# Three down-projection rounds by seven products in a two-layer hybrid decoder kernel, with the plain rounds accumulated onto the residual in PSUM

## The chip, the cores and the metric

The kernel runs on one core of a Trainium2 chip. The metric is the device time of one execution in microseconds. The kernel before took 1250.43 us (median of 3 runs, 1250.01 to 1251.3).

## What is computed

Two layers of a hybrid decoder on 528 tokens (16 meta tokens and 512 real ones), model width 1024. Each layer is an attention part (a combined input projection, forgetting attention, retention, an output projection) and a feed-forward part, which is where the change lies:

```python
hn = rmsnorm(h, ffn_norm_g)
ff = jax.nn.silu(jnp.einsum('bld,df->blf', hn, w_gate)) * jnp.einsum('bld,df->blf', hn, w_up)
return h + jnp.einsum('blf,fd->bld', ff, w_down)
```

The feed-forward width is 2816. The last layer needs the 512 real tokens only.

## The kernel before

Everything is kept transposed, with 128 features on the partitions and the tokens along the free axis: the residual is eight tiles h0 to h7 of 128x528. Each float32 matrix product is made of three: both operands are split into a rounded part (hi) and the remainder (lo), and TensorE (PE) multiplies hi by hi, hi by lo and lo by hi. A split costs one ScalarE (ACT) copy for hi and one VectorE (DVE) subtraction for lo; weights are split in the kernel as well, after their load.

The feed-forward part (`ffn`, L861) goes through the 22 blocks of 128 hidden features, f = 0 to 21, in six rounds, `ROUNDS` (L27). Blocks 0 and 1 are plain. Each later block is a `Unit` (L1055) that computes gate and up together by a seven-product scheme on 2x2 blocks: four sets of weight combinations are made from the gate tile `raw` and the up tile `fraw` (`make1` to `make4`, sums into a tile `S`), and PE consumes them in `head` (24 matmuls: 12 into a bank x, 12 into the bank pair zy), `middle` (36) and `tail` (24). At the end of `tail`, `done` (L1127) adds zy to saved parts on DVE (L1131, "done" below), applies silu, multiplies and splits the block's activation (tiles ah, al).

When a round of blocks is complete, its down projection is added to h while the next round's units run: unit by unit, one of four pairs of output tiles (p = 0 to 3). A *plain* fill (`down`, L1181) multiplies the blocks of the round straight into a PSUM tile and adds that to h on DVE (L1202, L1204). A *seven-product* fill (`Pair`, L992) halves a pair of outputs, a round and the tokens, and needs seven products d[0] to d[6] of 6 matmuls each instead of 48 matmuls. It prepares its own weight combinations on DVE (L1012, L1013, L1018, L1020 and splits), and adds six partial results to h (L1039, L1041). It also needs four combinations of the activations of the round, the *forms* 1 to 4 (`token_forms`, L963). They are stored in places that are free then: form 1 in the second half of an activation tile, forms 2 and 3 in the second halves of the x tiles (xh, xl), form 4 in sqh, sql. `SEVENTHS` (L29) names the rounds whose fill is by seven products: rounds 2 (blocks 6 to 9, filled under units 10 to 13) and 4 (blocks 14 to 17, filled under units 18 to 21). Rounds 0, 1 and 3 are plain; the last round ends the layer.

Order. PE runs in the order of the program text (`steps`). On the other engines a scheduler places the instructions at build time, earlier text first, those under `high_priority` ahead; on the chip each engine runs its list in that fixed order and an instruction that waits holds up those behind it. Weight sets are made one to five jobs ahead (`need`, L935) and held in rings of two and three buffers. PSUM has eight banks: two pairs (psd) and four single ones (psa).

"Unit f", "layer 0" and "layer 1" below are these; "stage f" is the time from the done of unit f to the done of unit f+1.

Of the kernel before, what the change touches and what calls it, by code (L numbers as in the profile page):

```python
# [16 lines left out]
NK = D // 128  # L17
# [8 lines left out]
NF = DFF // 128  # L26
ROUNDS = ((0, 2), (2, 6), (6, 10), (10, 14), (14, 18), (18, 22))  # L27
PLAIN = 2
SEVENTHS = (2, 4)  # L29
SEVEN = (0, 1, 2, 3)  # L30
HB = NK // 2
EPS = 1e-6
# [9 lines left out]
def hybrid_kernel(ctx, tc, x_t, w_in, w_fl, w_out, w_gate, w_up, w_down, vecs, b_fg, rope, decay, mask, ident, out_t):  # L42
    nc = tc.nc
# [9 lines left out]
    h = [state.tile([128, T], F32, name=f"h{k}") for k in range(NK)]  # L53
# [100 lines left out]
    def split(hi, lo, src, pinned=False):  # L154
        return [pin(f, pinned).ins for f in (nc.scalar.copy(hi, src), nc.vector.tensor_sub(lo, src, hi.bitcast(F32)))]
# [116 lines left out]
    def psum():  # L272
        return psd.tile([128, 2, 512], F32, name="psd", tag="psd")

    def psum_a():
        return psa.tile([128, 512], F32, name="psa", tag="psa")
# [584 lines left out]
    def ffn(l, st, real, last):  # L861
        QC = REAL if real else FULL
        t0 = META if real else 0
        w = (T - t0) // 2
        HC = ((t0, t0 + w), (t0 + w, T))
# [4 lines left out]
        halves, forms = {}, {}  # L870

        def two(t):
            return t[:, t0:T].rearrange("p (a b) -> p a b", a=2)
# [89 lines left out]
        def token_forms(f, u2):  # L963

            r = seventh(f)[0]
            f0 = ROUNDS[r][0]
            k = (f - f0) % 2
            first = [two(t)[:, 1] for t in acts[f0 + k]]
            if f - f0 < 2:
                halves[k] = u2  # L970
                nc.vector.tensor_sub(u2[:, 0], u2[:, 1], u2[:, 0])
                split(*first, u2[:, 0])
                forms[r, 1, k] = first
                return
            if k == 0:
                forms[r] = [tt("sqh", F32R), tt("sql", F32R)]
            (a, b), (c, d) = ([t[:, i] for i in range(2)] for t in (halves.pop(k), u2))
            four = [two(t)[:, k] for t in forms[r]]
            second, third = ([two(t)[:, 1] for t in st["x"][i]] for i in (2 + k, k))
            for n, o, x, y, (hi, lo) in ((3, b, d, b, third), (2, d, d, a, second), (4, c, c, d, four)):  # L980
                with tc.high_priority() if k and n < 4 else ExitStack():
                    nc.vector.tensor_sub(o, x, y)
                    split(hi, lo, o)
                forms[r, n, k] = hi, lo

        def form(r, n):
            return lambda k: forms[r, n, k]
# [190 lines left out]

            return add_job(load=load, make=lambda hi, lo: splits(hi, lo, t["r"][:, 0:2 * n]), n=2 * n)

        def down(j, s, m, f0, f1, banks):  # L1181

            n = f1 - f0
            ps = []

            def chunk(k):
                def go():
                    if k == 0:
                        need(j)
                        ps.append([psum_a() for _ in HC] if banks else psum())  # L1190
                    t = ps[0] if banks else [ps[0][:, b] for b in range(2)]
                    cols = QC if real and not banks else HC
                    _, hi, lo = jobs[j]["w"][0]
                    fh, fl = acts[f0 + k]
                    for i, (a, b) in enumerate(((hi, fh), (hi, fl), (lo, fh))):
                        for v, (c0, c1) in zip(t, cols):
                            nc.tensor.matmul(v[:, 0:c1 - c0], a[:, s * n + k, :], b[:, c0:c1],  # L1197
                                             start=(k == 0 and i == 0), stop=(k == n - 1 and i == 2))
                    if k == n - 1:
                        if banks:  # L1200
                            for v, (c0, c1) in zip(t, HC):
                                nc.vector.tensor_add(h[m][:, c0:c1], v[:, 0:c1 - c0], h[m][:, c0:c1])  # L1202
                        else:
                            nc.vector.tensor_add(sv(h[m], real), pv(ps[0], real), sv(h[m], real))  # L1204
                return go
            return [chunk(k) for k in range(n)]

        def own():
            return [(NK, wring("fwhi"), wring("fwlo"))]
# [1 line left out]
        steps = []  # L1211
        fills = []
        units = {}
        for r, (f0, f1) in enumerate(ROUNDS):
            for f in range(f0, f1):
# [10 lines left out]
                u = units[f]  # L1226
                p, g0, g1 = fills.pop(0)
                seven = r - 1 in SEVENTHS and p in SEVEN
                after = r - 1 in SEVENTHS and p + 1 in SEVEN or r in SEVENTHS and f == f1 - 1 and 0 in SEVEN
                if seven:  # L1230
                    pair = Pair(r - 1, p)
                    u.rest()
                    pair.rest()
                    u.last()
                    jobs[u.w3]["reach"] = 5 if after else 4
                    d, m, t = pair.steps(), u.middle(), u.tail()
                    steps += d[0] + m[:NK] + d[2] + m[NK:] + d[1] + d[3] + t[:HB] + d[4] + t[HB:] + d[5] + d[6]
                    continue
                u.rest()
                steps += u.middle()  # L1240
                j = down_job(p, g0, g1)
                jobs[j]["reach"] = 4 if after else 3
                steps += down(j, 0, 2 * p, g0, g1, not real or f < PLAIN + 2)
                u.last()
                steps += u.tail()
                steps += down(j, 1, 2 * p + 1, g0, g1, f == PLAIN)
            fills = [(p, f0, f1) for p in range(NK // 2)]
        n = f1 - f0
        js = [down_job(p, f0, f1) for p, _, _ in fills]
# [8 lines left out]
        else:  # L1258
# [22 lines left out]
            for c0, c1 in (PA, PB):  # L1281
                for m in range(NK):
                    ps = []
# [343 lines left out]
```

## Time and profile before

| | |
|---|---|
| median of 3 runs | 1250.43 us (1250.01 to 1251.3) |
| span of the profiled execution | 1248.2 us |
| outside that span, by the median | 2.2 us |
| PE busy | 1236.6 us (99%), 9387 matmuls |
| DVE busy | 1062.2 us (85%), 2033 instructions |
| ACT busy | 733.5 us (59%) |
| done of unit 9, layer 0 and layer 1 | 420.39 us, 1031.76 us |

The profiled execution's own time outside the span is not recorded; the median is taken for it. A busy time of PE counts matmuls that overlap, so 99% says that PE hardly ever stood still, not how fast it went. The granted clock (PEclk) is 1.00 where PE runs at its full clock.

### The profile page before, as it was taken

How to read it: one execution, taken by the hardware profiler on the slowest of the kernel's cores; microseconds unless marked ns; L12 is line 12 of the kernel's file. 1: busy time of each engine (PE TensorE's matmuls, PEld its weight loads, DVE VectorE, ACT ScalarE, POOL GpSimd, SP SyncE). 2: the span in 40 equal slices, each digit the busy share in tenths (PEclk: the TensorE clock that was granted, in tenths of full speed). 3: DMA queues.
4: the chain of work that ended last, by engine and by line, in shares of the span. 5: the costliest groups of instructions: out<-in, count | busy, mean ns of one | idle time of the engine just before them, and what ended most of it. 6: DMA issues, size and time to landing. Idle time of an engine off the chain costs nothing.

```text
span 1248.2 us, 24164 instructions
## 1 busy us (share of the span) xinstructions
PE 1236.6 (99%) x9387; PEld 1192.1 (96%) x9387; DVE 1062.2 (85%) x2033; ACT 733.5 (59%) x1397; POOL 294.6 (24%) x568
## 2 busy tenths in 40 slices
PE   9999999999999999999999999999999999999997
PEld 9999999999999999999999989999799999999996
DVE  7887756889997999899876877568999989998996
ACT  7767655776544555455566766567765445454554
POOL 4555655440000000000035556554400000000000
PEclk9999999999999999999999999999999999999999
DMA  6222222222433233322312222231414333333322
GB/s 238 68 77 69 78 69 85 60 85 72 133 119 102 85 102 118 103 86 85 114 65 85 63 84 75 68 94 52 141 54 135 111 102 102 100 104 102 102 69 69
DMA packets 43347, 116.25 MB, mean 93 GB/s; under 512 B 5088, under 2 KB 9952, under 8 KB 43232
## 3 DMA queue, kind: packets, MB, share of 16 engines
q1 hardware_dynamic: 42800, 114.41, 28.8%
q8 instruction: 74, 1.21, 0.4%
q14 instruction: 41, 0.34, 0.1%
q10 hardware_dynamic: 432, 0.29, 0.1%
HBM read 112.58 MB, written 2.10 MB: 92 GB/s over the span
## 4 chain that ended last, share of the span: by engine, by line
PE 90%; DVE 5%; ACT 2%; DMA 1%; issue 1%; SPq 0%; ACTq 0%; DVEq 0%
PE psd L231 28%; PE psa L953 22%; PE psd L953 15%; PE psd L1197 8%; PE psa L231 5%; PE psa L1197 3%; PE psa L452 2%; PE psa L619 2%; PE psa L549 1%; PE psa L753 1%; PE psa L789 1%; DMA raw<-w_down 1%; DVE wlo L942 1%; DVE fwlo L942 0%; PE psa L312 0%
## 5 line engine op out<-in xcount | busy, mean ns | idle before, releaser
L208 POOL TENSOR_TENSOR wlo<-raw,whi 128x128 fp32r<-128x128 f32 x488 | 254.6, 557 | 212.2 <-ACT whi L204 212.2
L231 PE MATMUL psd<-xh,whi 128*128 128x264 f32 (+1 forms) x696 | 169.7, 313 | 0.0
L231 PE MATMUL psd<-xh,wlo 128*128 128x264 f32 (+1 forms) x696 | 161.0, 301 | 0.0
L231 PE MATMUL psd<-xl,whi 128*128 128x264 f32 (+1 forms) x696 | 160.6, 300 | 0.0
L231 PEld LDWEIGHTS psd<-xh,whi 128*128 128x128 f32 x696 | 112.6, 190 | 3.3 <-ACT whi L204 0.3
L231 PEld LDWEIGHTS psd<-xh,wlo 128*128 128x128 f32 x696 | 111.1, 188 | 4.4
L231 PEld LDWEIGHTS psd<-xl,whi 128*128 128x128 f32 x696 | 111.7, 189 | 2.5
L941 ACT CAST fwhi<-raw 128x512 fp32r<-128x512 f32 (+2 forms) x88 | 66.2, 757 | 72.3 <-PE psd L953 28.7
L204 ACT CAST whi<-raw 128x512 fp32r<-128x512 f32 (+1 forms) x140 | 82.1, 612 | 32.5 <-PE psd L231 17.3
L127 POOL MEMSET kc<- 64x528 f32 x4 | 2.1, 534 | 367.5 <-PE psd L1197 367.3
L942 DVE TENSOR_TENSOR fwlo<-raw,fwhi 128x512 fp32r<-128x512 f32 (+2 forms) x88 | 75.1, 854 | 7.5 <-ACT fwhi L941 7.4
L941 ACT CAST whi<-raw 128x1024 fp32r<-128x1024 f32 (+2 forms) x72 | 56.8, 789 | 37.6 <-PE psd L953 21.1
L1117 ACT COPY e<-psa 128x264 f32<-128x264 f32 (+1 forms) x120 | 44.9, 374 | 53.5 <-PE psa L953 51.9
L953 PE MATMUL psa<-th,fwhi 128*128 128x264 f32 (+1 forms) x248 | 70.4, 284 | 0.0
L953 PE MATMUL psa<-tl,fwhi 128*128 128x264 f32 (+1 forms) x248 | 70.1, 283 | 0.0
L953 PE MATMUL psa<-th,fwlo 128*128 128x264 f32 (+1 forms) x248 | 70.1, 283 | 0.0
L953 PE MATMUL psa<-th,whi 128*128 128x264 f32 (+1 forms) x232 | 65.4, 282 | 0.0
L942 DVE TENSOR_TENSOR wlo<-raw,whi 128x1024 fp32r<-128x1024 f32 (+1 forms) x72 | 64.1, 893 | 1.5 <-ACT whi L941 1.4
L953 PE MATMUL psa<-tl,whi 128*128 128x264 f32 (+1 forms) x232 | 65.4, 282 | 0.0
L953 PE MATMUL psa<-th,wlo 128*128 128x264 f32 (+1 forms) x232 | 65.3, 281 | 0.0
L566 ACT ACTIVATE pr<-pr,nmax 128x144 f32<-128x144 f32 (+1 forms) x64 | 36.8, 575 | 45.7 <-DVE nmax L553 26.3
L941 ACT CAST fwhi<-S 128x1024 fp32r<-128x1024 f32 (+1 forms) x34 | 28.8, 846 | 34.0 <-PE psa L953 14.3
(442 smaller groups left out, 4381.7 us busy)
## 6 DMA issues: line engine op xcount, KB each, us to landing
raw<-w_in SPq DMA_DIRECT2D x54, 512.0 KB, 3.5
raw<-w_gate SPq DMA_DIRECT2D x44, 512.0 KB, 3.5
fraw<-w_up SPq DMA_DIRECT2D x40, 512.0 KB, 3.5
raw<-w_down SPq DMA_DIRECT2D x80, 256.0 KB, 3.7
raw<-w_out SPq DMA_DIRECT2D x16, 512.0 KB, 3.5
h<-x_t SPq DMA_DIRECT2D x8, 264.0 KB, 4.5
dec<-decay SPq DMA_DIRECT2D x8, 264.0 KB, 2.7
raw<-w_up SPq DMA_DIRECT2D x4, 512.0 KB, 3.9
```

The source lines that it names most:

```text
L204: pin(nc.scalar.copy(hi, job["raw"][:, c0:c1]), pinned)
L208: pin(sub(lo[:, c:c + step], job["raw"][:, c0 + c:c0 + c + step], hi[:, c:c + step].bitcast(F32)), pinned)
L231: nc.tensor.matmul(ps[1][b][:, 0:c1 - c0], w[:, wk, :], x[:, c0:c1], start=(k == 0 and i == 0), stop=(k == n - 1 and i == 2))
L452: nc.tensor.transpose(ps[:, 128 * j:128 * j + 128], src[:, o:o + 128], idt)
L549: nc.tensor.matmul(sc[0:nq, 0:c1 - c0], qq[:, q0:q0 + nq], kk[:, c0:c1], start=(i == 0), stop=(i == 1))
L566: nc.scalar.activation(pr, pr, AF.Exp, bias=nmax[0:nq], scale=-1.0, accum_out=rsum)
L619: nc.tensor.matmul(po[:, c0:SEQ], v[:, j, :], pp[:, j, META + c0:T], start=(j == 0 and i == 0), stop=(j == 4))
L941: nc.scalar.copy(hi, src)
L942: nc.vector.tensor_sub(lo, src, hi.bitcast(F32))
L953: nc.tensor.matmul(bank()[:, 0:b.shape[-1]], a[:, o + k, :], b, start=(fresh and k == 0 and i == 0), stop=(k == n - 1 and i == 2), skip_gr ...
L1117: nc.scalar.copy(self.t["e"][:, i], self.t["x"][:, 0:w])
L1197: nc.tensor.matmul(v[:, 0:c1 - c0], a[:, s * n + k, :], b[:, c0:c1], start=(k == 0 and i == 0), stop=(k == n - 1 and i == 2))
```

## The change

1. `SEVENTHS` becomes (1, 2, 4): round 1 (blocks 2 to 5) is filled by seven products, under units 6 to 9.
2. Rounds 1 and 2 now follow each other, so that the forms of round 2 would overwrite those of round 1 while round 1's last fill still reads them. For round 2, forms 2 to 4 are therefore taken out of `token_forms` and made under unit 9: steps `later_forms` stand in the program behind the last product that reads the old form (forms 2 and 3 of the first half behind d[1] and d[4], those of the second half at the done of unit 9, form 4 behind d[6]).
3. Plain fills under units (now rounds 0 and 3) are `kept`: ACT copies h into the PSUM tile first (`place`, between the two parts of `middle` for the first output and between those of `tail` for the second), the matmuls accumulate onto it, and ACT copies the sum back into h. The DVE add goes. Their matmuls now always use half the tokens each: in layer 1, where a bank takes 512 columns, that is two matmuls of 256 for each one of 512.

The core of the diff:

```diff
-SEVENTHS = (2, 4)
+SEVENTHS = (1, 2, 4)
...
-            if k == 0:
+            halves[k] = halves[k], u2
+            if r - 1 not in SEVENTHS:
+                for n in (3, 2, 4):
+                    later_form(r, n, k)
+            elif k:
+                for n in (2, 3):
+                    later_form(r, n, k)
+
+        def later_form(r, n, k):
+            (a, b), (c, d) = ([t[:, i] for i in range(2)] for t in halves[k])
+            if n == 4 and k == 0:
                 forms[r] = [tt("sqh", F32R), tt("sql", F32R)]
...
+            o, x, y = {2: (a, d, a), 3: (b, d, b), 4: (c, c, a)}[n]
+            hi, lo = [two(t)[:, k] for t in forms[r]] if n == 4 else [two(t)[:, 1] for t in st["x"][k if n == 3 else 2 + k]]
+            with tc.high_priority() if k and n < 4 else ExitStack():
+                nc.vector.tensor_sub(o, x, y)
+                split(hi, lo, o)
+            forms[r, n, k] = hi, lo
+
+        def later_forms(r, n, *ks):
+            return [lambda k=k: later_form(r, n, k) for k in ks] if r in SEVENTHS and r - 1 in SEVENTHS else []
...
+            def place():
+                ps.append([psum_a() for _ in HC] if banks else psum())
+                with tc.high_priority():
+                    if banks:
+                        for v, (c0, c1) in zip(ps[0], HC):
+                            nc.scalar.copy(v[:, 0:w], h[m][:, c0:c1])
+                    else:
+                        nc.scalar.copy(ps[0][:, :, 0:w], two(h[m]))
...
-                    cols = QC if real and not banks else HC
+                    cols = QC if real and not banks and not kept else HC
...
-                                             start=(k == 0 and i == 0), stop=(k == n - 1 and i == 2))
+                                             start=(k == 0 and i == 0 and not kept), stop=(k == n - 1 and i == 2), skip_group_check=kept)
...
+                        if kept:
+                            with tc.high_priority():
+                                if banks:
+                                    for v, (c0, c1) in zip(t, HC):
+                                        nc.scalar.copy(h[m][:, c0:c1], v[:, 0:w])
+                                else:
+                                    nc.scalar.copy(two(h[m]), ps[0][:, :, 0:w])
...
-                    steps += d[0] + m[:NK] + d[2] + m[NK:] + d[1] + d[3] + t[:HB] + d[4] + t[HB:] + d[5] + d[6]
+                    i = r if f == f1 - 1 else None
+                    steps += (d[0] + m[:NK] + d[2] + m[NK:] + d[1] + later_forms(i, 2, 0) + d[3] + t[:HB] + d[4]
+                              + later_forms(i, 3, 0) + t[HB:] + d[5] + d[6] + later_forms(i, 4, 0, 1))
...
+                (p0, d0), (p1, d1) = (down(j, s, 2 * p + s, g0, g1, b, True)
+                                      for s, b in enumerate((not real or f < PLAIN + 2, f == PLAIN)))
+                m, t = u.middle(), u.tail()
+                steps += m[:NK] + [p0] + m[NK:] + d0 + t[:HB] + [p1] + t[HB:] + d1
```

How the lists of the engines change at three places. **DVE, layer 0, around the done of unit 9.** Before, these are the last rows of stage 8 and the first of stage 9; fwlo_5958 is the lo part of the second weight set of unit 10, L1131 the done of unit 9:

```order
L1202 TENSOR_TENSOR h6_79<-psa_5859,h6_79 128x264
L1098 TENSOR_TENSOR raw_5838<-raw_5838,S_5959 128x512
L1012 TENSOR_TENSOR S_6063<-raw_6058 128x256
L1013 TENSOR_TENSOR S_6063<-S_6063,raw_6058 128x256
L1018 TENSOR_TENSOR raw_6058<-raw_6058 128x256
L942 TENSOR_TENSOR fwlo_5958<-S_5959,fwhi_5957 128x1024
L1131 TENSOR_TENSOR sg_5910<-psd_5774,e_5772 128x528
L942 TENSOR_TENSOR fwlo_6006<-raw_5846,fwhi_6005 128x512
```

Now the same weight set is fwlo_6033, and these are the rows up to it; ahead of them, after the done of unit 9 (L1142 now), stand another 12 instructions (four of 128x528, two of 128x512, six of 128x264), the done itself counted. xl, sql and L990 are forms of round 2:

```order
L1150 TENSOR_TENSOR tq_5996<-e_5834,tq_5996 128x264
L155 TENSOR_TENSOR sql_6025<-tq_5792,sqh_6024 128x264
L990 TENSOR_TENSOR tq_5591<-tq_5996,tq_5591 128x264 x2
L155 TENSOR_TENSOR al1_6001<-tq_5996,ah1_6000 128x528
L155 TENSOR_TENSOR xl3_4158<-tq_5591,xh3_4157 128x264
L155 TENSOR_TENSOR xl1_4150<-tq_5591,xh1_4149 128x264
L990 TENSOR_TENSOR tq_5996<-tq_5996,tq_5591 128x264
L1096 TENSOR_TENSOR S_6034<-S_6034,raw_5907 128x512
L155 TENSOR_TENSOR sql_6025<-tq_5996,sqh_6024 128x264
L1103 TENSOR_TENSOR fraw_5909<-raw_5907,fraw_5909 128x512
L1029 TENSOR_TENSOR raw_5915<-raw_5915 128x256
L942 TENSOR_TENSOR fwlo_6033<-S_6034,fwhi_6032 128x1024
```

The weight set stood one row ahead of the done of unit 9; it now ends with the 25th instruction from that done on.

**DVE, layer 1, around the done of unit 8.** Before, wlo_13206 is the lo part of the second weight set of unit 9:

```order
L1012 TENSOR_TENSOR S_13358<-raw_13353 128x256
L1013 TENSOR_TENSOR S_13358<-S_13358,raw_13353 128x256
L1018 TENSOR_TENSOR raw_13353<-raw_13353 128x256
L1204 TENSOR_TENSOR h4_77<-psd_13179,h4_77 128x512
L942 TENSOR_TENSOR wlo_13206<-S_13207,whi_13205 128x1024
L1131 TENSOR_TENSOR sg_13224<-psd_13107,e_13105 128x512
```

Now it is wlo_13515; two instructions, the done of unit 8 (L1142) and an add of 128x512, stand ahead of these rows:

```order
L1024 TENSOR_TENSOR S_13422<-S_13422,raw_13417 128x256
L1052 TENSOR_TENSOR h5_78<-psa_13356,h5_78 128x256
L1144 SCALAR_TENSOR_TENSOR sg_13488<-sg_13488,R_12068 128x512
L942 TENSOR_TENSOR fwlo_13421<-S_13422,fwhi_13420 128x512
L1095 TENSOR_TENSOR S_13516<-fraw_13411 128x512
L1147 SCALAR_TENSOR_TENSOR tq_13492<-sg_13488,R_12068 128x512
L1096 TENSOR_TENSOR S_13516<-S_13516,raw_13409 128x512
L1052 TENSOR_TENSOR h6_79<-psa_13554,h6_79 128x256
L1149 TENSOR_TENSOR tq_13492<-psa_13323,tq_13492 128x256
L1150 TENSOR_TENSOR tq_13492<-e_13336,tq_13492 128x256
L1103 TENSOR_TENSOR fraw_13411<-raw_13409,fraw_13411 128x512
L942 TENSOR_TENSOR wlo_13515<-S_13516,whi_13514 128x1024
```

It moved from one row ahead of the done of unit 8 to the 14th instruction from that done on.

**ACT, layer 1, under unit 15 (a plain fill).** Before, from the silu of unit 14 on:

```order
L441 ACTIVATE sg_14362<-sg_14362 128x512
L1117 COPY e_14409<-psa_14396 128x256
L155 CAST ah6_14370<-tq_14366 128x256
L1117 COPY e_14409<-psa_14396 128x256
L941 CAST fwhi_14509<-S_14511 128x1024
L941 CAST whi_14479<-raw_14475 128x1024
L155 CAST ah6_14370<-tq_14366 128x256
L1117 COPY e_14409<-psa_14396 128x256
```

Now, with the copies of h into PSUM (L1204) and back (L1227) for the fill's two outputs h2 and h3:

```order
L441 ACTIVATE sg_14671<-sg_14671 128x512
L1204 COPY psd_14776<-h2_75 128x2x256
L1128 COPY e_14729<-psa_14716 128x256
L941 CAST fwhi_14844<-S_14846 128x1024
L155 CAST ah6_14679<-tq_14675 128x256
L1128 COPY e_14729<-psa_14716 128x256
L941 CAST whi_14801<-raw_14797 128x1024
L155 CAST ah6_14679<-tq_14675 128x256
L1128 COPY e_14729<-psa_14716 128x256
L1227 COPY h2_75<-psd_14776 128x512
L1204 COPY psd_14842<-h3_76 128x2x256
```

The second output's copy into PSUM stands right behind the first output's copy back; both outputs use the same pair of banks.

More of the change, by code (lines that the diff above doesn't have):

```diff
@@ L974, in token_forms @@
                 return
-            if k == 0:
-                forms[r] = [tt("sqh", F32R), tt("sql", F32R)]
[L977 to L984, printed above, removed]
+            halves[k] = halves[k], u2
[8 more added lines that the diff above has]
+            if n == 4 and k == 0:
+                forms[r] = [tt("sqh", F32R), tt("sql", F32R)]
+            o, x, y = {2: (a, d, a), 3: (b, d, b), 4: (c, c, a)}[n]
[6 more added lines that the diff above has]
+            return [lambda k=k: later_form(r, n, k) for k in ks] if r in SEVENTHS and r - 1 in SEVENTHS else []
         def form(r, n):
@@ L1179, in down_job, with down @@
             return add_job(load=load, make=lambda hi, lo: splits(hi, lo, t["r"][:, 0:2 * n]), n=2 * n)
-        def down(j, s, m, f0, f1, banks):
+        def down(j, s, m, f0, f1, banks, kept=False):
             n = f1 - f0
             ps = []
+            def place():
[6 more added lines that the diff above has]
+                        nc.scalar.copy(ps[0][:, :, 0:w], two(h[m]))
             def chunk(k):
@@ L1189, in go @@
                         need(j)
-                        ps.append([psum_a() for _ in HC] if banks else psum())
+                        if not kept:
+                            ps.append([psum_a() for _ in HC] if banks else psum())
                     t = ps[0] if banks else [ps[0][:, b] for b in range(2)]
-                    cols = QC if real and not banks else HC
+                    cols = QC if real and not banks and not kept else HC
                     _, hi, lo = jobs[j]["w"][0]
@@ L1197, in go @@
                             nc.tensor.matmul(v[:, 0:c1 - c0], a[:, s * n + k, :], b[:, c0:c1],
-                                             start=(k == 0 and i == 0), stop=(k == n - 1 and i == 2))
+                                             start=(k == 0 and i == 0 and not kept), stop=(k == n - 1 and i == 2), skip_group_check=kept)
                     if k == n - 1:
-                        if banks:
+                        if kept:
[5 more added lines that the diff above has]
+                                    nc.scalar.copy(two(h[m]), ps[0][:, :, 0:w])
+                        elif banks:
                             for v, (c0, c1) in zip(t, HC):
@@ L1205, in chunk @@
                 return go
-            return [chunk(k) for k in range(n)]
+            steps = [chunk(k) for k in range(n)]
+            return (place, steps) if kept else steps
         def own():
```

4 lines of the change are left out of this document (removed).

## The prediction

> **What bounds the kernel now.** I read the page first, then the feed-forward stages by windows, then the lists of PE and DVE in order of time. The busy line and the chain by engine:
>
> ```profile
> PE 1236.6 (99%) x9387; PEld 1192.1 (96%) x9387; DVE 1062.2 (85%) x2033; ACT 733.5 (59%) x1397; POOL 294.6 (24%) x568
> ...
> PE 90%; DVE 5%; ACT 2%; DMA 1%; issue 1%; SPq 0%; ACTq 0%; DVEq 0%
> ```
>
> PE sets the end, so fewer or cheaper matmuls should show in full as long as nothing else falls behind. Whether it does is read by stage. Three windows of layer 0, from done to done: units 6 and 7 (plain fills), units 8 and 9 (plain fills, and the forms of round 2), units 10 to 13 (seven-product fills). After the length, each pair of columns is an engine's busy time and its count, PE, PEld, DVE, ACT, POOL; then the clock:
>
> ```profile
> 372.21:404.34 32.13, 32.13 (x267) 32.13 (x266) 25.68 (x43) 14.41 (x23) 0.00 (x0) 1.00 0.33 99
> 404.34:436.54 32.20, 32.20 (x267) 32.20 (x266) 32.14 (x62) 16.49 (x31) 0.00 (x0) 1.00 0.28 83
> 436.54:497.89 61.35, 61.35 (x506) 61.35 (x505) 60.98 (x107) 31.75 (x49) 0.00 (x0) 1.00 0.33 105
> ```
>
> PE is busy throughout; but in the second and the third row DVE is too: 32.14 of 32.20 and 60.98 of 61.35 us. DVE has room only under plain fills without forms (6.4 us in the first row). Both engines are full, and the change takes from one and gives to the other in the very stages 6 to 9.
>
> **Part 1: matmuls.** The spacing of matmuls, from the first and the last of runs of 264 columns (28 matmuls), of 256 (36) and of 512 (8):
>
> ```profile
> 445.82 0.28 PE L953 MATMUL psa<-th,fwhi 128*128 128x264 f32 x1
> ...
> 449.11 0.29 PE L953 MATMUL psa<-th,fwhi 128*128 128x264 f32 x1
> ...
> 1109.78 0.28 PE L953 MATMUL psa<-xl,fwhi 128*128 128x256 f32 x1
> ...
> 1113.91 0.28 PE L953 MATMUL psd<-th,whi 128*128 128x256 f32 x1
> ...
> 1116.61 0.39 PE L1197 MATMUL psd<-al,whi 128*128 128x512 f32 x1
> ...
> 1118.23 0.40 PE L1197 MATMUL psd<-ah,wlo 128*128 128x512 f32 x1
> ```
>
> That is 3.29/27 = 0.122, 4.13/35 = 0.118 and 1.62/7 = 0.231 us. Layer 0: round 1 falls from 4 pairs x 48 = 192 matmuls to 4 x 42 = 168, so 24 x 0.122 = 2.9 us less. Layer 1: round 1 was 96 of 512 columns (22.2 us) and becomes 168 of 256 (19.8 us), 2.4 us less. Against that the `kept` fills of layer 1 cut 30 (round 0) and 96 (round 3) matmuls of 512 columns into two of 256 each: 126 x (0.236 - 0.231) = 0.6 us more. **PE work: -4.7 us.**
>
> **Part 2: DVE in stages 6 to 9.** DVE's price of an instruction, where it is never idle, is the step from one start to the next:
>
> ```profile
> 419.25 1.22 DVE L942 TENSOR_TENSOR fwlo<-S,fwhi 128x1024 fp32r<-128x1024 f32 x1
> 420.39 0.70 DVE L1131 TENSOR_TENSOR sg<-psd,e 128x528 f32<-128x528 f32 x1
> 421.01 0.68 DVE L942 TENSOR_TENSOR fwlo<-raw,fwhi 128x512 fp32r<-128x512 f32 x1
> 421.61 0.70 DVE L1133 SCALAR_TENSOR_TENSOR sg<-sg,R 128x528 f32<-128x528 f32 x1
> ...
> 424.40 0.42 DVE L1138 TENSOR_TENSOR tq<-psa,tq 128x264 f32<-128x264 f32 x1
> 424.75 0.42 DVE L1139 TENSOR_TENSOR tq<-e,tq 128x264 f32<-128x264 f32 x1
> 425.08 1.22 DVE L942 TENSOR_TENSOR wlo<-fraw,whi 128x1024 fp32r<-128x1024 f32 x1
> 426.22 0.42 DVE L982 TENSOR_TENSOR tq<-tq 128x264 f32<-128x264 f32 x1
> ...
> 1030.62 1.23 DVE L942 TENSOR_TENSOR fwlo<-S,fwhi 128x1024 fp32r<-128x1024 f32 x1
> 1031.76 0.68 DVE L1131 TENSOR_TENSOR sg<-psd,e 128x512 f32<-128x512 f32 x1
> 1032.36 0.68 DVE L942 TENSOR_TENSOR fwlo<-raw,fwhi 128x512 fp32r<-128x512 f32 x1
> ...
> 1033.56 0.42 DVE L942 TENSOR_TENSOR fwlo<-raw,fwhi 128x256 fp32r<-128x256 f32 x1
> 1033.89 0.68 DVE L1204 TENSOR_TENSOR h<-psd,h 128x512 f32<-128x512 f32 x1
> ```
>
> So 1.14 us for 1024 elements, 0.62 for 528, 0.60 for 512, 0.34 for 264 and for 256 (0.33 to 0.35).
>
> First the balance. A seven-product fill needs three lo parts of 512 and one of 256, four sums of 256, one add of 528 and five of 264 (3 x 0.60 + 10 x 0.34 + 0.62 = 5.8 us); a plain one a lo part of 1024 and two adds of 528 (2.4 us). Four units take 3.4 us more each, 13.7 us. In layer 0 the first two windows hold 57.8 us of DVE work; that becomes 71.5, against PE's 64.3 - 2.9 = 61.4 us. So DVE comes out about 10 us short, less what it is ahead at the start. The adds that go to ACT (two per plain fill) are freed in stages 2 to 5 and 14 to 17, where they buy a lead of a few weight sets at most, since the rings hold no more.
>
> Where it shows is read from the list. DVE cannot start on the done of a unit before PE has finished that unit's tail, so what stands behind the done in DVE's list runs after it. In layer 0 the lo part of unit 10's second weight set ends with the 25th instruction from the done of unit 9: five of 528, four of 512, fifteen of 264 or 256, one of 1024, or 3.10 + 2.40 + 5.10 + 1.14 = 11.7 us. In that time PE has, after the tail of unit 9, d[5] and d[6] (12 matmuls), the head of unit 10 (24), d[0] (6) and the two hi products (2): 44 x 0.122 = 5.4 us. Then it needs that lo part. **Stall 6.4 us.** In layer 1 the same list has eight of 512, fourteen of 256 and one of 1024 (xl of form 2 slipped ahead of the done): 4.8 + 4.7 + 1.1 = 10.6 against 44 x 0.118 = 5.2 us, **stall 5.4 us**. One unit earlier, layer 1: two instructions and the twelve rows of the second place, that is eight of 512, five of 256, one of 1024: 7.6 against 5.2 us, **stall 2.4 us**; in layer 0 there: four of 528, three of 512, one of 264, one of 1024: 5.8 against 5.4, **stall 0.4 us**. Stages 6 and 7 still make their second set in time (3.3 us behind the done in layer 0).
>
> Each stall has two handovers on top. PE's last matmul into zy to DVE's start on it, with DVE waiting for PE; and, at the end of layer 1, a DVE instruction that PE waits for and PE's start (DVE's and PE's rows):
>
> ```profile
> 436.21 0.28 PE L953 MATMUL psd<-xh,wlo 128*128 128x264 f32 x1
> ...
> 436.54 0.70 DVE L1131 TENSOR_TENSOR sg<-psd,e 128x528 f32<-128x528 f32 x1
> ...
> 1220.24 0.69 DVE L155 TENSOR_TENSOR al<-tq,ah 128x512 fp32r<-128x512 f32 x1 [0.69 <-ACT ah L155]
> ...
> 1220.99 0.39 PE L953 MATMUL psd<-al,whi 128*128 128x272 f32 x1 [0.34 <-DVE al L155]
> ```
>
> 0.33 us from the start of the last matmul, of which my sum has 0.12; 0.06 us from the end of the DVE row; and the end of a lo part is 0.08 us behind its step (1.22 against 1.14). That makes 0.35 us a stall. The four stalls are 6.7 + 5.8 + 2.8 + 0.7 = **+16.0 us**. Behind each the later sets of the unit are late by less than PE by then is, and the done of unit 10 is about as late on DVE as on PE (23 against 21.8 us), so I add nothing there. While DVE waits behind its list, ACT's hi part of the same set waits too (its sum S is ready 1.3 us ahead of the lo part); no other engine hurts.
>
> **Part 3: PE's clock after a stall.** The stalls of stage 9 leave PE idle for 4 to 5 us at a stretch. No such gap stands in the middle of this trace, but its two ends show what idleness does. After the last matmuls (first row), and from the first ones on:
>
> ```profile
> 1238.84 1.38 PE L1345 MATMUL psa<-S,ones 128*128 128x240 f32 x6
> ...
> 1240.00:1242.00 2.00, 0.21 (x2) 1.00 0.66 223
> 1242.00:1244.00 2.00, 0.00 (x0) 0.71 0.64 226
> 1244.00:1246.00 2.00, 0.00 (x0) 0.50 1.04 340
> ...
> 1.59 4.21 PE L1458 MATMUL psa<-wide,ones 128*128 128x512 f32 x9 [1.59 <-DVE wide L64]
> 5.60 0.64 PE L231 MATMUL psd<-xh,whi 128*128 128x264 f32 x2
> 6.04 0.64 PE L231 MATMUL psd<-xl,whi 128*128 128x264 f32 x2
> ...
> 7.31 0.40 PE L231 MATMUL psd<-xl,whi 128*128 128x264 f32 x2
> 7.55 0.40 PE L231 MATMUL psd<-xh,wlo 128*128 128x264 f32 x2
> ```
>
> The clock (the number behind the count) falls to half at about 1242.8, 2.6 us after PE's last work at 1240.2. At the start two matmuls of 264 take 0.44 us until about 7.2, 5.6 us after the first matmul, and 0.24 afterwards. If a stall of 4 to 5 us halves the clock and it comes back as slowly, 5.6 us pass at 0.22 instead of 0.122 us a matmul: 5.6 x 0.445 = 2.5 us lost a stall. PE is the later engine then, so nothing covers it. I take it for the two stalls of stage 9: **+5.0 us**; bounds 0 (no fall) and 7.5 (layer 1's stall of stage 8 too).
>
> [...]
>
> **Part 4: the copies on ACT.** A copy of h into PSUM is not in the trace. Its nearest rows are a cast within SBUF and a copy out of PSUM of 512 elements; the first row is the longest job that can stand ahead of it:
>
> ```profile
> L941 ACT CAST whi<-raw 128x1024 fp32r<-128x1024 f32 x32 | 33.7, 1052 | 16.3 <-PE psd L953 7.9 <-ACT whi L941 2.2 <-ACT e L1117 2.1
> ...
> L941 ACT CAST whi<-raw 128x512 fp32r<-128x512 f32 x32 | 19.9, 621 | 20.9 <-PE psd L953 13.2 <-issue 5.1 <-PE psa L1197 2.2
> ...
> L797 ACT COPY d<-psa 128x512 f32<-128x512 f32 x8 | 4.7, 582 | 1.1 <-PE psa L786 0.9
> ```
>
> So 0.58 to 0.62 us either way. ACT is 45% busy in these windows (14.41 of 32.13). The tightest place is layer 1, where both outputs use one pair of banks: copy back 0.58, copy in 0.62 and some 0.3 of handovers are 1.5 us, under the tail's 24 x 0.118 = 2.8 us. One cast of 1.05 us in front still fits. I take 0; if two casts stood in front, 0.8 us at each of six units (4, 5, 14 to 17), so 0 to +4.8. The forms of round 1 in stages 2 to 5 (16 DVE instructions of 264, 5.4 us) go where twelve adds (5.2 us) leave: 0. No DMA is added, and SP's list is as long as before.
>
> **Sum.** -4.7 + 16.0 + 5.0 = +16.3 us. The profiled span of 1248.2 becomes 1264.5, and with the 2.2 us around it the median of 1250.43 becomes **1266.7**.
>
> **Rivals.** *Stalls without a lower clock* (0.25): the idle stretches are cut by the two hi products in between and the clock stays. 1250.4 - 4.7 + 16.0 = 1261.7. For it: one end-of-program case is all that I have. *DVE hides it* (0.05): the second set of unit 10 is ready in time after all and PE keeps its 4.7 us: 1245.7. This decides if DVE has done 25 instructions within 5.4 us of the done; the rows say 11.7, and lists are not reordered on the chip, so little speaks for it. *ACT's copies come late too* (0.08): 16.3 + 4.8, 1271.5; against it ACT's idle half. *The stalls are about half as long* (0.07), since some DVE steps go faster while PE stands: 1250.4 - 4.7 + 8.0 = 1253.7. The forecast keeps 0.55, with its own range of 1263 to 1273 (a shorter return of the clock, or three falls and an ACT wait).
>
> **Chances and range.** Two cases (0.12) lie outside 1258 to 1273, and a tenth of the others with their unknowns, which leaves about 8 in 10 inside. Faster by over 0.2% (2.5 us, about what a measurement here can tell): 0.05, the second rival; within: 0.02, the short end of the fourth; slower: 0.93.
>
> **What would show it.** Right: PE waits of 4 to 7 us with DVE's fwlo L942 as releaser (or ACT's cast that waits for the same S) shortly after the done of unit 9 in both layers, a wait of some 3 us one unit earlier in layer 1, PEclk under 1.00 behind them, no PE wait at plain fills. Wrong: DVE idle in stages 8 and 9, PE at 0.122 us a matmul through them (1245.7), or waits of PE on psd or psa copies from ACT at L1218.

## The result: 1267.92 us, 1.4% slower

| | before | after |
|---|---|---|
| median | 1250.38 us (1250.01 to 1251.3) | 1267.92 us (1266.96 to 1269.03) |
| ratio, 95% interval | | 1.0141 (1.0128 to 1.0154) |
| span of the profiled execution | 1248.2 us | 1265.8 us (its own time 1267.51) |

The time was forecast at 1266.7 us. On the page after, the busy line, the clock by slices and the chain by engine:

```profile
PE 1239.5 (98%) x9561; PEld 1202.4 (95%) x9561; DVE 1079.3 (85%) x2105; ACT 779.5 (62%) x1525; POOL 293.6 (23%) x568
...
PEclk9999999999999899999999999999999998999999
...
PE 89%; DVE 7%; ACT 2%; DMA 2%; issue 0%; SPq 0%; DVEq 0%; ACTq 0%
```

These hardly differ from before: two slices of the clock show an 8, and DVE's share of the chain went from 5 to 7%. The stages tell more. The three windows of layer 0 that the prediction shows, from done to done (stages 6 and 7, stages 8 and 9, stages 10 to 13), and then the two stretches of half clock (after the length come PE, PEld, DVE, ACT, POOL, then the clock):

```profile
372.48:403.36 30.88, 30.88 (x255) 30.88 (x254) 30.64 (x59) 14.62 (x26) 0.00 (x0) 1.00 0.31 96
403.36:444.07 40.71, 33.83 (x254) 33.05 (x253) 39.29 (x77) 19.64 (x35) 0.00 (x0) 0.92 0.27 83
444.07:505.33 61.26, 61.26 (x505) 61.26 (x504) 61.04 (x105) 32.60 (x54) 0.00 (x0) 1.00 0.33 106
429.37:436.20 6.83, 5.30 (x22) 5.00 (x23) 6.83 (x13) 3.77 (x6) 0.00 (x0) 0.50 0.35 85
1050.60:1057.42 6.82, 5.98 (x26) 5.69 (x27) 6.47 (x12) 3.32 (x7) 0.00 (x0) 0.50 0.38 96
```

Stages 6 and 7 got 1.25 us shorter (32.13 before), as fewer matmuls should make them. Stages 8 and 9 got 8.5 us longer (32.20 before), and there PE is no longer the full engine: DVE works 39.29 of 40.71 us, PE 33.83. DVE's work in these four stages grew from 57.8 to 69.9 us.

Here is the place of the loss in layer 0. First PE: the last matmul before the stall, and the waits behind it; then DVE from the done of unit 9 (first row) to the lo part that PE needs, and ACT's cast that PE waits for (last row).

```profile
424.48 0.28 PE L953 MATMUL psa<-ah,fwlo 128*128 128x264 f32 x1
430.42 0.59 PE L953 MATMUL psa<-th,fwhi 128*128 128x264 f32 x1 [5.66 <-ACT fwhi L941]
430.81 0.42 PE L953 MATMUL psa<-tl,fwhi 128*128 128x264 f32 x1
431.71 0.59 PE L953 MATMUL psa<-th,fwlo 128*128 128x264 f32 x1 [0.48 <-DVE fwlo L942]
432.09 0.42 PE L953 MATMUL psa<-th,fwhi 128*128 128x264 f32 x1
432.31 0.42 PE L953 MATMUL psa<-tl,fwhi 128*128 128x264 f32 x1
```

```profile
419.66 0.71 DVE L1142 TENSOR_TENSOR sg<-psd,e 128x528 f32<-128x528 f32 x1
...
428.21 0.42 DVE L990 TENSOR_TENSOR tq<-tq 128x264 f32<-128x264 f32 x1
428.56 0.68 DVE L1096 TENSOR_TENSOR S<-S,raw 128x512 f32<-128x512 f32 x1
429.16 0.42 DVE L155 TENSOR_TENSOR sql<-tq,sqh 128x264 fp32r<-128x264 f32 x1
429.50 0.68 DVE L1103 TENSOR_TENSOR fraw<-raw,fraw 128x512 f32<-128x512 f32 x1
430.10 0.41 DVE L1029 TENSOR_TENSOR raw<-raw 128x256 f32<-128x256 f32 x1
430.44 1.21 DVE L942 TENSOR_TENSOR fwlo<-S,fwhi 128x1024 fp32r<-128x1024 f32 x1
...
429.32 1.05 ACT L941 CAST fwhi<-S 128x1024 fp32r<-128x1024 f32 x1 [0.25 <-DVE S L1096]
```

DVE is never idle from the done to the lo part; L990 and L155 are the forms. PE's wait is put down to ACT, but ACT only waits for the sum S of L1096, which stands behind the forms. From done to lo part it is 12.0 us (11.7 were summed up). Behind the wait the matmuls come every 0.22 us, not 0.12.

Measured between the starts of the last matmuls of the units' tails, in layer 0 stage 8 took 16.45 us and stage 9 24.36, where 126 matmuls without a wait take 15.36; in layer 1 stage 8 took 17.84 and stage 9 23.07, against 14.87. The excesses are 1.1 + 9.0 + 3.0 + 8.2 = 21.3 us.

### The profile page after: what moved, and what is told of

It is laid out like the page before. It is cut to its first block, busy times and chain, and to the rows that moved or that the text cites. A ratio compares the mean times of both kernels' runs of the same rounds, so it can differ in the third digit from the quotient of the medians.

```text
span 1265.8 us, 24734 instructions
## 1 busy us (share of the span) xinstructions
PE 1239.5 (98%) x9561; PEld 1202.4 (95%) x9561; DVE 1079.3 (85%) x2105; ACT 779.5 (62%) x1525; POOL 293.6 (23%) x568
## 4 chain that ended last, share of the span: by engine, by line
PE 89%; DVE 7%; ACT 2%; DMA 2%; issue 0%; SPq 0%; DVEq 0%; ACTq 0%
PE psd L231 28%; PE psa L953 24%; PE psd L953 17%; PE psd L1218 5%; PE psa L231 5%; PE psa L452 2%; PE psa L1218 2%; PE psa L619 2%; PE psa L549 1%; PE psa L753 1%; PE psa L789 1%; DMA raw<-w_in 1%; DVE fwlo L942 1%; DMA raw<-w_down 0%; DVE wlo L942 0%
## 5 line engine op out<-in xcount | busy, mean ns | idle before, releaser
L941 ACT CAST fwhi<-raw 128x512 fp32r<-128x512 f32 (+2 forms) x100 | 70.6, 714 | 52.8 <-PE psd L953 30.2
L942 DVE TENSOR_TENSOR fwlo<-raw,fwhi 128x512 fp32r<-128x512 f32 (+2 forms) x100 | 79.8, 800 | 10.6 <-ACT fwhi L941 10.3
L953 PE MATMUL psa<-th,fwlo 128*128 128x264 f32 (+1 forms) x248 | 71.5, 288 | 1.0 <-DVE fwlo L942 1.0
L953 PEld LDWEIGHTS psa<-th,fwhi 128*128 128x128 f32 x248 | 47.7, 192 | 11.0 <-ACT fwhi L941 10.6
```

The source lines that it names most:

```text
L953: nc.tensor.matmul(bank()[:, 0:b.shape[-1]], a[:, o + k, :], b, start=(fresh and k == 0 and i == 0), stop=(k == n - 1 and i == 2), skip_gr ...
```

## The experiments

Theory: VectorE has more to do in stages 8 and 9 than these last, since round 1's seven-product fills and round 2's forms meet there; the copies on ScalarE cost nothing. Rivals: the copies and the cut matmuls (e1, e2), the mere order of VectorE's list (e3), and for the five us of half clock, that they are no loss of their own (e5, e6).

**e1, the plain fills alone.**

```diff
-SEVENTHS = (1, 2, 4)
+SEVENTHS = (2, 4)
```

> Only the plain fills change: rounds 2 and 4 stay the rounds of seven products, as before, and the plain down rows are placed into PSUM and taken out of it by ScalarE. Theory (the loss is VectorE's queue behind the forms of rounds 1 and 2, the copies cost nothing): no wait of TensorE over 1 us in the feed-forward stages, granted clock 1.0 through the units; only layer 1's plain fills, cut into pairs of 256 columns, add time: 222 matmuls of 512 become 444 of 256, by the prediction's price (0.6 us for 126) about +1.1 us, so 1251.4 us. Rival (ScalarE's copies at the head and the end of a fill hold TensorE up): 96 fills of two copies with a fraction of a microsecond each, 1255 us or more, with waits on the copies (L1206 or L1229) ahead of the plain matmuls.

Measured 1254.52 us (1253.12 to 1255.58), ratio 1.003 (1.0019 to 1.0041): the forecast of 1251.4 failed. No PE wait names a copy, and layer 0's feed-forward part is as long as before to 0.1 us in every unit; so the rival falls as well. The profiled execution (1255.58 us, the longest of seven) has its excess in three places. It reaches layer 0's units 1.2 us later, by a wait in the first input projection; that differs from execution to execution (1.2 us in e4's trace too, and -0.1 to 0.8 us in the others) and is not shown to come of the edit. Layer 1's units with plain fills take 1.7 us more by the starts of their last matmuls (1.1 was forecast). And at the end of layer 1 2.6 us go, where DVE's done comes late (rows of DVE, ACT and PE):

```profile
1217.45 1.23 DVE L942 TENSOR_TENSOR fwlo<-raw,fwhi 128x1024 fp32r<-128x1024 f32 x1 [2.34 <-ACT fwhi L941]
1218.59 0.69 DVE L1142 TENSOR_TENSOR sg<-psd,e 128x512 f32<-128x512 f32 x1
...
1216.37 1.05 ACT L941 CAST fwhi<-raw 128x1024 fp32r<-128x1024 f32 x1 [2.88 <-DMA raw<-w_down]
...
1219.33 0.39 PE L953 MATMUL psd<-ah,whi 128*128 128x272 f32 x1 [1.85 <-DVE sg L1142]
```

With fewer adds, the scheduler put the next fill's lo part ahead of the done in DVE's list; it waits for ACT's cast, and that for a DMA. Behind the wait the clock halves for 3.41 us (from 1219.98), which is part of the 2.6. The changed kernel has no such wait there. So no wait shows the copies themselves as a price, but the order that the edit gives DVE's list can be one.

**e2, the third round alone.**

```diff
-                (p0, d0), (p1, d1) = (down(j, s, 2 * p + s, g0, g1, b, True)
+                d0, d1 = (down(j, s, 2 * p + s, g0, g1, b)
...
-                steps += m[:NK] + [p0] + m[NK:] + d0 + t[:HB] + [p1] + t[HB:] + d1
+                steps += u.middle() + d0 + u.tail() + d1
```

> The third round of seven products with its later forms stays, the plain fills go back to PSUM of their own and VectorE's add onto the residual. Theory: the stalls come of the forms, so they stand here as in the changed kernel, and somewhat longer, since VectorE has the adds of rounds 0 and 3 back; TensorE saves 5.3 us of matmuls (24 x 0.122 in layer 0, 24 x 0.119 less the 126 that are not cut in layer 1), the stalls take 16 to 20 us and the half clock 5: 1266 to 1271 us. Rival (the copies and the cut matmuls make the loss): the saving of the products alone, 1245 us.

Measured 1277.69 us (1276.19 to 1279.61), ratio 1.0218 (1.0202 to 1.0233). The stalls stand, and there are more of them (who waited for whom: us in total, how often, the longest):

```profile
PE psa L953 <- ACT fwhi L941: 13.1, 3, 6.1
PE psa L953 <- DVE fwlo L942: 5.3, 4, 2.2
PE psa L953 <- DVE wlo L942: 2.9, 2, 2.2
```

Earlier stages are now late as well: against the changed kernel 2.7 us in stages 5 and 6 of layer 0, and in layer 1 6.2 us in stage 5 and 4.0 in stage 7 (stage 8 is 3.1 us shorter there). So the copies on ScalarE don't make the loss, they save 10 us of it. I had the direction, but mis-sized how full VectorE is in stages 5 to 7: the forecast of 1266 to 1271 us failed.

**e3, order instead of quantity.**

```diff
-                with tc.high_priority() if self.f == PLAIN else ExitStack():
+                with tc.high_priority() if self.f in (PLAIN, 9, 10) else ExitStack():
                     nc.vector.tensor_add(s[:, HB:NK], b[:, 0:HB], b[:, HB:NK])
```

> As the changed kernel, but the second weight set of units 9 and 10 (its sums and its split, L1092 to L1096) is put ahead on VectorE, so that the forms of round 2 come behind it. Theory of quantity (VectorE has more work in these stages than the stage lasts, and what is put back is late next): the stall of unit 10 gets shorter or goes, another stands in the next sets (by the sums of measured steps up to 4.3 us in unit 9's or 3.5 us in layer 1), in all 1256 to 1263 us with less time at half clock. Theory of order (only the place of the forms ahead of that set matters): the stalls go and the products' saving is left, 1246 to 1248 us.

Measured 1270.45 us (1270.19 to 1271.22), ratio 1.016 (1.0145 to 1.0175): even slower than the change. The list of PE's waits:

```profile
PE psa L953 <- ACT whi L941: 5.3, 2, 3.0
PE psa L953 <- DVE wlo L942: 2.6, 4, 0.8
PE psa L953 <- DVE fwlo L942: 2.3, 3, 0.8
PE psd L953 <- DVE al L155: 2.0, 2, 1.4
PE psd L953 <- ACT ah L155: 1.9, 2, 1.6
```

The wait of 5.7 us is gone, but the third sets (whi, wlo) and the activations and forms themselves (ah, al) are late in its place. In layer 1 stage 9 ends 3.5 us earlier than in the changed kernel and stage 10 gives back 5.9. What is put back is late next, as quantity has it; other orders were not run. The forecast of 1256 to 1263 us failed, since I had counted the sets of weights only.

**e4 and e8, work moved to GpSimd.** e4 moves 78 instructions, e8 40 (rounds `(1,)`, units 7 to 10).

```diff
-                nc.vector.tensor_add(s[:, 2:4], r[:, 4:6], r[:, 6:8])
...
+                e = nc.gpsimd if self.r in (1, 2) else nc.vector
+                e.tensor_add(s[:, 2:4], r[:, 4:6], r[:, 6:8])
...
-                nc.vector.tensor_sub(a[:, HB:NK], a[:, HB:NK], s[:, 0:HB])
+                (nc.gpsimd if self.f in (7, 8, 9, 10, 11, 12, 13) else nc.vector).tensor_sub(a[:, HB:NK], a[:, HB:NK], s[:, 0:HB])
```

> As the changed kernel, but GpSimd does the pair sums of rounds 1 and 2 (L1023, L1024, L1029, L1031) and the difference of the fourth weight set of units 7 to 13 (L1109), which were VectorE's: some 2 to 3 us per stage leave VectorE. Theory of quantity: every set is then ready 1.5 us or more ahead of TensorE by the sums of measured steps, no wait over 1 us, no half clock, so the products' saving shows: 1245.5 to 1247 us, below the kernel before. Rival (the forms are late whatever is ahead of them, or GpSimd's 1 to 2 us for each sum puts the sets behind as far as VectorE did): waits on the sets of weights stay, 1255 us or more.

> The run with GpSimd, at a lower dose: pair sums of round 1 alone and the fourth set's difference of units 7 to 10 alone (40 instructions on GpSimd, not 78). That run showed VectorE's instructions between two SBUF tiles at 1.2 to 1.75 us, not 0.69 to 1.22, beside GpSimd's: 21 us lost again in all. If the small waits that were left there (5.6 and 7.7 us) come of GpSimd's company, half of it gives shorter ones in stages 5 to 7 and 11 to 13, but less relief in stages 8 to 10: 1255 to 1260 us. If the relief decides, the waits of stage 9 come back by 1 to 2 us per layer: 1261 to 1265 us.

e4: 1260.37 us (1260.14 to 1261.33), ratio 1.0078 (1.0061 to 1.0094). e8: 1265.03 us (1262.67 to 1267.07), ratio 1.0124 (1.0107 to 1.014). In e4 the long stalls are gone (the longest wait of a unit is 1.4 us, on `h L1054`), and the clock stays at 1.00 throughout. But ten waits of 0.3 to 1.4 us are left in the feed-forward stages. DVE's and GpSimd's rows at one place of e4 (with e4's own line numbers, two further down):

```profile
988.29 0.69 DVE L1098 TENSOR_TENSOR S<-S,raw 128x512 f32<-128x512 f32 x1
988.88 0.42 DVE L1054 TENSOR_TENSOR h<-psd,h 128x256 f32<-128x256 f32 x1
989.22 1.75 DVE L942 TENSOR_TENSOR fwlo<-raw,fwhi 128x512 fp32r<-128x512 f32 x1
990.89 0.68 DVE L942 TENSOR_TENSOR fwlo<-S,fwhi 128x512 fp32r<-128x512 f32 x1
991.49 1.21 DVE L1105 TENSOR_TENSOR fraw<-raw,fraw 128x512 f32<-128x512 f32 x1
...
989.11 1.32 POOL L1111 TENSOR_TENSOR raw<-raw,S 128x512 f32<-128x512 f32 x1 [13.51 <-ACT fwhi L941]
991.11 1.04 POOL L1033 TENSOR_TENSOR raw<-raw,S 128x256 f32<-128x256 f32 x1 [0.69 <-DVE fwlo L942]
```

A subtraction of 512 elements takes 0.68 us alone and 1.75 and 1.21 beside GpSimd, which of its 36 us of relief (64 x 0.42 + 14 x 0.68) takes 21 back (every row that overlapped GpSimd's against the median of its shape alone: 9.5 us in layer 0 and 11.5 in layer 1). So e4 supports quantity (less work, no long stall), while its own forecast of 1246 failed for a price that I had left out. e8 has its waits at wlo again (6.0 us in three, in stage 10 of both layers and stage 12 of layer 1, not in stage 9 as expected) and landed at the top of the second case, which is nearer to the relief deciding than to GpSimd's company.

**e5 and e6, the stall filled with matmuls.**

```diff
+                        v = psum_a()
...
+                            nc.tensor.matmul(v[:, 0:w], hi[:, 0, :], x, start=True, stop=True)
...
+                        d[0].append(lambda n=34 if real else 40, go=idle: go(n))
```

> As the changed kernel, with extra matmuls of 264 (256) columns into a bank that nobody reads, put right ahead of the first matmul that waits in the stage of unit 10: 40 of them in layer 0 (40 x 0.122 = 4.9 us of the 5.9), 34 in layer 1 (4.1 us of the 4.8). Theory (the idle time makes the clock fall, and the half clock is a loss of its own of 2.5 to 2.8 us per layer): the granted clock stays 1.0, the matmuls behind the wait come at 0.12 us, 1262 to 1263.5 us. Rival (VectorE stays the bound behind the wait, so that at full clock TensorE only waits again for the next sets): clock 1.0, but new waits behind, 1266 to 1268.5 us. If the idle time isn't what lowers the clock: 0.22 us spacing as before, 1268 us.

> The same with half as many extra matmuls: 20 in layer 0 (2.4 us, some 3.5 us of the wait left idle), 17 in layer 1 (2.0 us, 2.8 left). It asks how much idle time it takes: in the run without ScalarE's copies a wait of 2.5 us in layer 0 went by at full clock and waits of 2.4 us in layer 1 did not. If 2.5 to 3.5 us is enough, the clock falls in at least one layer and the time is 1264 to 1268 us; if it takes more than 3.5 us, 1262 to 1263.5 us.

e5: 1266.56 us (1265.92 to 1266.99), ratio 1.013 (1.0115 to 1.0145). PE in layer 0's stall; then stage 9 of both layers by windows:

```profile
424.68 5.00 PE L1272 MATMUL psa<-ah,fwhi 128*128 128x264 f32 x40
430.51 0.39 PE L953 MATMUL psa<-th,fwhi 128*128 128x264 f32 x1 [0.83 <-ACT fwhi L941]
...
431.79 0.39 PE L953 MATMUL psa<-th,fwlo 128*128 128x264 f32 x1 [0.78 <-DVE fwlo L942]
```

```profile
420.00:444.30 24.30, 22.70 (x184) 22.27 (x183) 24.16 (x47) 12.36 (x22) 0.00 (x0) 1.00 0.22 72
1042.00:1064.70 22.70, 21.36 (x179) 20.95 (x178) 22.64 (x44) 12.30 (x21) 0.00 (x0) 1.00 0.23 70
```

The idle time does lower the clock: with PE fed, it stays at 1.00. Stage 9 gets 2.0 and 2.3 us shorter, so the half clock cost 4.3 us where it stood. But at full clock PE meets the next limit: stage 12 of layer 1 gives back 1.2 us (a wait of 0.76 on DVE's wlo; e6 has the same). Stages 3 and 4 of layer 1, ahead of the filled stall, take 0.9 us more, with two waits of 0.2 us on ACT's copies e; why they come is not shown. By the medians 1.4 us are left of the gain, which lies in the rival's range; the theory's 1262 to 1263.5 us failed.

e6: 1268.46 us (1265.87 to 1270.55), ratio 1.0145 (1.0129 to 1.016). Layer 0 before and after the fall of the clock, and layer 1's stall:

```profile
424.80:431.65 6.85, 2.96 (x23) 2.54 (x21) 6.85 (x17) 4.07 (x7) 0.00 (x0) 1.00 0.00 0
431.65:435.07 3.42, 3.30 (x15) 3.30 (x16) 2.74 (x5) 0.95 (x4) 0.00 (x0) 0.50 0.31 92
1047.00:1064.00 17.00, 13.66 (x114) 13.25 (x113) 16.94 (x31) 9.24 (x14) 0.00 (x0) 1.00 0.32 94
```

A gap of 3.5 us (from start to start of matmuls, as all gaps here) halves the clock for 3.42 us in layer 0, one of 2.8 us in layer 1 does not. This execution (1265.87 us) is the shortest of four; the others have a mean clock of 0.991 to 0.995 (0.998 here), so more falls, and the median lies above the 1264 to 1268 us that were forecast for a fall.

Length alone doesn't tell: a gap of 2.2 us did it in e10, one of 2.4 in e8 did not. Where the gap lies does, in these runs. In every trace with more than one fall these lie whole steps of 3.413 us apart (429.37 and 1050.60 in the changed kernel: 621.23 us = 182 x 3.4133; the 6.83 us that its clock is at half each time are two such steps). Here are e10's step that ends with a fall, at 473.95, and then the two steps of e8 that hold its gap, counted from e8's fall at 1094.04:

```profile
470.54:473.95 3.41, 1.51 (x11) 1.16 (x10) 3.33 (x7) 2.27 (x3) 0.00 (x0) 1.00 0.00 0
...
1056.49:1059.91 3.42, 1.92 (x16) 1.70 (x14) 3.42 (x8) 2.83 (x4) 0.00 (x0) 1.00 0.00 0
1059.91:1063.32 3.41, 2.76 (x23) 2.76 (x24) 3.41 (x6) 1.15 (x4) 0.00 (x0) 1.00 0.01 5
```

e10's gap lies within one step, and PE is busy for 1.51 of 3.41 us in it; e8's is spread over two, which keeps both above that (1.92 and 2.76). The gap of 2.8 us in e6 is spread as well, over steps with 1.59 and 1.90 us of work.

**e7, forms 2 and 3 of round 2 left out.**

```diff
+            if r != 2 or n == 4:
+                with tc.high_priority() if k and n < 4 else ExitStack():
```

> As the changed kernel, but forms 2 and 3 of round 2 are not computed (the products that need them read what lies in their place, so the output is not the reference's; form 4 stays). It takes 8 instructions of 256 columns, 3.4 us, off VectorE per layer in stages 8 and 9. Theory of quantity: the stall of stage 9 shortens by about that (6.5 to some 3 us in layer 0, 5.4 to some 2 to 3 us in layer 1), the half clock goes or shrinks: 1255 to 1261 us. Rival (the sets are late for another reason): 1266 us or more. If all of the loss were these forms, 1246 to 1248 us.

Measured 1265.24 us (1262.13 to 1267.21), ratio 1.0118 (1.0101 to 1.0134). Stage 9 alone behaves as the theory says, 6.5 us shorter in layer 0 and 7.7 in layer 1, with no half clock there in layer 0. But stages 11 and 12 of layer 0 give 2.2 us back, and stages 8, 10 and 12 of layer 1 9.3 us, with a half clock of 3.41 us behind the wait in each of these three. VectorE's debt goes on into the stages of round 2's own fills, which have no room to pay it. The forecast of 1255 to 1261 failed on that.

**e9, e10 and e12, less of the third round.** These put round 1's first two (e9, e12) or three pairs on seven products and its other pairs on plain fills, so that no or fewer such fills meet the forms of round 2:

```diff
+PART = {1: (0, 1)}
...
-            if r - 1 not in SEVENTHS:
+            if True:
...
-                seven = r - 1 in SEVENTHS and p in SEVEN
+                seven = r - 1 in SEVENTHS and p in PART.get(r - 1, SEVEN)
```

The second edit puts the forms of round 2 back to the place that they had before the change, so these three differ from the changed kernel in that too. In all three, round 1's plain fills read form 1 where the second token half of blocks 2 and 3 would have to be (e12's expectation is wrong in calling it the whole computation). A version with these halves kept would need their splits besides; it wasn't run. e9, e10 and e11 also have 512-column fills onto placed rows in layer 1, and with them do not compute the reference's result there; how it goes wrong is not shown.

> Half of the third round: only the first two pairs of round 1 go by seven products (in units 6 and 7), its last two row pairs are plain fills placed by ScalarE; the forms of round 2 are then made where they were before the change, and layer 1's plain fills keep their 512 columns. Theory of quantity: the pairs and the forms of round 2 no longer meet in units 8 and 9, by the sums of measured steps every set is 1.5 us or more ahead of TensorE, so no wait over 1 us and no half clock; half the products' saving is left, 12 matmuls per layer, 1.46 + 1.43 us: 1247 to 1248.5 us, below the kernel before. If the third round costs by itself (its sums and adds in units 6 and 7): half of the loss or more, 1254 us and up.

> The same with three of round 1's four pairs by seven products (units 6, 7 and 8; one plain fill in unit 9). Theory of quantity: the products save 4.3 us in all; by the sums of measured steps sets are late by 0.4 and 1.8 us in layer 0 and by 2.4, 0.6 and 1.8 us in layer 1 (each 0.35 us more by the handover), and after a wait near 2.4 us the clock may fall: 1252 to 1257 us. If it is a matter of a few instructions' order and not of quantity, it lies with the half (1246 to 1248 us) or with the whole (1267 us).

> Half of the third round again (the first two pairs of round 1 by seven products), with the whole computation of the reference: ScalarE's placement in 256 columns for layer 0's plain fills and for layer 1's rounds 0 and 1; round 3 of layer 1 has its plain fills in PSUM of their own and VectorE's add, as before the change. Theory: the products save 1.39 us in layer 0 and 1.43 us in layer 1, the cut matmuls of layer 1's rounds 0 and 1 cost 0.3 + 0.45 us by the first run without the third round, no wait over 1 us in the feed-forward stages: 2 us below the kernel before, 1248 to 1249.5 us. Rival (placement itself or the end of the kernel takes the rest back, as the 2.6 us at the end of that run): 1250 to 1251 us, no difference.

e9: 1249.38 us (1248.5 to 1250.11), ratio 0.9991 (0.9982 to 1.0). e10: 1259.71 us (1257.62 to 1261.49), ratio 1.0072 (1.0057 to 1.0088). e12: 1249.38 us (1248.54 to 1250.05), ratio 0.9992 (0.9983 to 1.0001). Stages 8 and 9 of layer 0 in e12, where the changed kernel stalls:

```profile
401.00:435.00 34.00, 34.00 (x282) 34.00 (x281) 32.89 (x60) 20.53 (x39) 0.00 (x0) 1.00 0.31 94
```

PE is full again, with no wait over 0.3 us in the feed-forward stages of e12, and VectorE has 1.1 us of room. In layer 0 the gain is there in full (1.39 us of 1.46); in layer 1 the cut matmuls and small waits spend it. With two pairs there is no stall, with three 9.3 us of loss, with four 17.5, which is how an engine that fills up would bend. e9 missed its range of 1247 to 1248.5 us and e12 landed in its own (1248 to 1249.5). e10 came out above its range (1252 to 1257), with a half clock in both layers; its waits stand in stages 10 and 12. No version was found that is clearly faster than the kernel before.

**e11, 512 columns again in the changed kernel's plain fills.**

```diff
-                        nc.scalar.copy(ps[0][:, :, 0:w], two(h[m]))
+                        nc.scalar.copy(pv(ps[0], real), sv(h[m], real))
...
-                    cols = QC if real and not banks and not kept else HC
+                    cols = QC if real and not banks else HC
```

> The changed kernel with layer 1's plain fills placed and multiplied in 512 columns where one bank holds the row (not 2 x 256). It takes away the cut of matmuls alone: the units of rounds 0 and 3 in layer 1 end 0.9 us earlier in all against the changed kernel (it measured +0.3 and +0.6 us there), ScalarE copies 512 columns in one instruction either way: 1267 us. Rival (the cut also spaced TensorE so that VectorE lagged less): the stalls take the 0.9 us back, 1267.9 us.

Measured 1267.59 us (1267.39 to 1268.0), ratio 1.0138 (1.0124 to 1.0152). Layer 1's stages with plain fills get 0.6 us shorter in all (0.1 in stages 3 to 5, 0.5 in stages 13 to 17), stage 7 of layer 1 takes 0.7 longer and stages 8 and 9 0.6 less. The difference from the changed kernel is within their spread, so that the two cases are not told apart; the cut is no cause of the loss.

## Why the prediction was right, step by step

- **PE's work, -4.7 us.** Right to some 0.6 us. Layer 0's feed-forward part took 7.3 us more in all, 10.1 us of excess less 2.8 (2.9 forecast); layer 1's took 9.83 more, 11.17 less 1.34 (1.8 forecast). Layer 1's stages with plain fills take 1.0 us more, where 0.6 was put for the cut of 126 matmuls. e11 gets 0.6 us back by undoing the cut, so that price held. The other 0.4 is mostly single steps at the first matmuls of a unit, 0.16 to 0.22 us in stages 3, 4 and 15 where 0.12 is usual; their cause is open.
- **The balance.** DVE's work in stages 6 to 9 of layer 0 was put at 71.5 us and is 69.9; the time of these stages, 71.6 us, is now DVE's. e2 (more on VectorE: 10 us slower), e4 and e7 (less), e9 and e10 (a smaller dose) confirm quantity, and in e3 the one other order that was run only moved the waits. That DVE's steps go faster while PE stands (the fourth rival) is not seen: the 25 steps came in the order of the list and took 12.0 us, where 11.7 were summed up.
- **Four stalls, +16.0 us, and half clock, +5.0.** Together 21.0 forecast, 21.3 measured. By stage: 0.7, 9.2, 2.8 and 8.3 us forecast; 1.1, 9.0, 3.0 and 8.2 measured. Of that e5 puts 4.3 us to the clock, and so 17.0 to the stalls: one term was 1.0 us too low and the other 0.7 too high, so that the sum is closer than its parts by luck.
- **"PE is the later engine then, so nothing covers it".** This held within stage 9, where feeding PE brought 4.3 us, and not over the kernel, where 1.4 us were left by the median: VectorE's debt stands close behind.
- **How the clock falls and comes back.** I took 5.6 us at half speed from the kernel's start. It was 6.83 us, two steps of 3.41, but PE was busy for only 5.30 and 5.98 us of them; that these lie so near to 5.6 is luck. The 2.6 us from PE's last work to the fall at the end of the kernel before do not show how much idle time it takes: the fall at 1242.85 ends a step of 3.41 us (from 1239.44) in whose first part PE still worked for 0.77 us. A shorter return of the clock, for which the forecast's range left room, is one such step, as e6 has it in layer 0 (3.42 us); in the changed kernel the stalls of stage 9 reach into the first step at half clock, and a second one followed.
- **ACT's copies, 0.** Right: no wait of PE is put down to them in the changed kernel's plain fills or in e1. That they would buy "a lead of a few weight sets at most" was too little: without them the time is 10 us longer.
- **What was not in the sum**: some 0.2 us at the start, 0.5 us in layer 1's attention part and 0.4 us in layer 1's stages with plain fills. They make most of the 1.2 us by which the forecast is low.

## What to carry to other kernels

When two engines are both full in a stage, a change that takes from one and gives to the other is read from the other's list: sum its steps from the event that it must wait for to the thing that the first engine needs, and set it against the first engine's work in the same stretch. If the second engine's total is over the stage's length, as here, one reordering or one relief does not help for long, since the debt shows at the next set (e3, e7); test it by dose (two, three and four pairs here) and not only by undoing. Before work is moved to an idle engine, ask what it does to the neighbour that it is taken from (in e4 it took back 21 of 36 us).

## What the runs showed of the hardware

- Ahead of the programs' ends, the half clock of PE came in stretches of 3.41 or 6.83 us only, 13 and 7 times over all the traces. With each trace cut into steps of 3.413 us by its own falls, from 20 us on, PE was busy for at most 0.46 of the step ahead of each of the 34 falls (14 of them at the ends), and for 0.47 or more of every step at full clock that no fall followed, but for one of 0.45 at the end of e6. So a step need not be wholly idle, and idle time of 1.9 us was enough where it lay within one (e10). Ahead of the ends, steps at half clock were the last where PE was busy for 0.86 of them or more, and another followed where it was busy for 0.75 or less.
- In e4, VectorE's instructions of 512 elements with two SBUF inputs took up to 1.75 us beside GpSimd's in place of 0.68, while those that read PSUM stayed at 0.42 to 0.43 (27 of 264 columns that overlapped in layer 0).
